# Attention and state space heads issued in pairs: scores of different rows in turn, transposes evicted by kind, products with v together

## The chip, the cores and the metric

One core of one Trainium2 chip runs the whole program in one launch. The metric is the device time of an execution in microseconds; the time of a kernel is the median of its runs.

## The reference

256 tokens of width 1024, batch 1, float32. The first block has two layers; each is a modulated RMS norm, a hybrid mixer, a residual, another norm, a squared-ReLU MLP, a residual. The mixer has three branches side by side, and the change touches all three:

```python
# differential attention: 4 heads, two maps of 32 columns each, v of 64
s1 = einsum('bqhd,bkhd->bhqk', q1b, k1) * scale; s2 = einsum(..., q2b, k2) * scale
p = _masked_softmax(s1, mask) - lam * _masked_softmax(s2, mask)
o = einsum('bhqk,bkhe->bqhe', p, v)
# MLA: 4 heads, scores from a 64-column and a 32-column (rotary) part, v of 64
sc = (einsum('bqhd,bkhd->bhqk', qnb, kn) + einsum('bqhr,bkr->bhqk', qrb, kr)) * scale
o = einsum('bhqk,bkhe->bqhe', _masked_softmax(sc, _chunk_mask(start, s)), v)
# state space (Mamba2): 8 heads of 64, state 64, two groups
scores = einsum('bclhn,bcshn->bhcls', cc, bc) * exp(where(causal, seg, -inf))
y_diag = einsum('bhcls,bcshp->bclhp', scores, xd)
```

The chunk mask lets a query see its own chunk of 64 keys and all earlier ones. The second block has one layer: a mixer of RWKV, moba attention (8 heads of 64 with ALiBi slopes, causal; with 256 tokens there is one block of keys) and an S5 state space branch, then a mixture of 32 experts.

## The kernel before

A class `Prog` emits the program; the Tile framework's scheduler orders each engine's instructions ahead of time by priorities and dependencies, which program order sets. Where `self.ordered` is on (`inorder`, `pin`), an instruction keeps its place in program order. So the code's order moves instructions, but the order on each engine is fixed before the run.

The large projections are "strips": a weight unit of 128 x 1024 comes by DMA (`raw`), ACT rounds it (`whi`), DVE takes the rest (`wlo`), and PE makes three products for each of eight blocks of 128 x 128 into a PSUM tile of tag `d` (`ps_d<-u,whi`, `ps_d<-xh,whi`, `ps_d<-u,wlo`). They stand between the attention steps. In the output projection they read `yh`/`xl` and accumulate into tiles of the tags `s` and `t`. The adaptive modulation's products (`ps_d<-raw,cnd_s`) are 32 columns wide, four column tiles beside each other.

PSUM in a mixer has eight banks: tags `d`, `s`, `t`, `o` with two each. One attention head or map goes like this:
- `scores` (L925): q against k into a tile of 128 x 384 of tag `s`, 128 columns for the first half of the queries and 256 for the second; head h reads rows 64a (MLA, moba) or 64a + 32m (diff) of the array. MLA adds a rotary product of 32 rows. `chunkmask` (L919) adds the mask with two bf16 products of one row.
- `soft` (L910): two reduces (L913, L914) and a scaling on DVE, two exps with sums on ACT (L378). A reciprocal and two multiplies on DVE follow; in diff attention two maps are combined with lambda (L1188 ff.).
- `pv` (L930): three transposes of 128 x 128 on PE (`tr`, L401) into a tile of tag `t`, one copy of 384 columns on ACT (`at_pT`), and two products with v into one half of the columns of `ps_o`.

`mla_head` (L1130) runs this four times one after the other; the diff loop (L1175) eight times, two maps to a `pv`; `moba` (L1641) eight times, with two slope products `mb_ak` of two rows and two masks of 128 rows in place of the chunk mask. The state space loop (L1225) goes head by head: an exponent product of 40 rows (`ps_s<-cs,i`), two masks, three exps (`ssE`), a multiply by `G` on DVE, two products with `xd` into one half of `ps_o`.

Every matmul goes through `mm` (L393), every ACT operation through `act` (L378, L379), DVE operations through `tt`, `ts`, `stt` (L382, L386, L390). So groups have these lines, and are told apart by their tiles.

Of the kernel before, what the change touches and what calls it, by code (L numbers as in the profile page):

```python
# [26 lines left out]
BF = mybir.dt.bfloat16  # L27
I32 = mybir.dt.int32
AF = mybir.ActivationFunctionType
OP = mybir.AluOpType  # L30
# [4 lines left out]
P = 128  # L35
T = 256
# [275 lines left out]
class Prog:  # L312
# [33 lines left out]
    def sb(self, pool, shape, tag, dt=F32, bufs=None):  # L346
        return pool.tile(shape, dt, name=tag, tag=tag, bufs=bufs)
# [568 lines left out]
        self.act(e[:, 0:P], sc[:, 0:P], AF.Exp, bias=mx[:, 0:1], scale=scale, accum=sm[:, j:j + 1])  # L916
        self.act(e[:, P:384], sc[:, P:384], AF.Exp, bias=mx[:, 1:2], scale=scale, accum=sm[:, j + 1:j + 2])

    def chunkmask(self, sc, r):  # L919

        for o in (0, 256):
            self.mm(sc[:, o:o + P], self.B("cm_q")[r:r + 1], self.B("cm_k")[r:r + 1], start=False, stop=True,
                    skip_group_check=True)

    def scores(self, sc, q, k, first, last=False):  # L925

        self.mm(sc[:, 0:P], q[:, 0:P], k[:, 0:P], start=first, stop=last, skip_group_check=True)
        self.mm(sc[:, P:384], q[:, P:T], k[:, 0:T], start=False, stop=last, skip_group_check=True)

    def pv(self, pool, p, v, vcol, o, half):  # L930

        tp = self.pt([P, 384], "t")
        for b in range(3):
            self.tr(tp[:, b * P:(b + 1) * P], p[:, b * P:(b + 1) * P])
        pT = self.sb(pool, [P, 384], "at_pT", bufs=2)

        self.act(pT, tp)
        oo = o[64 * half:64 * half + 64]
        self.mm(oo[:, 0:T], v[:, 0, vcol:vcol + 64], pT[:, 0:T], start=True, stop=False)
        self.mm(oo[:, P:T], v[:, 1, vcol:vcol + 64], pT[:, T:384], start=False, stop=True)  # L940


    def mixconst(self, l):
# [28 lines left out]
    def _mixer(self, pool, l, xT, pre, fill, n):  # L972
        nc = self.nc
        sb = lambda *a, **k: self.sb(pool, *a, **k)
# [4 lines left out]
        first = [("in", l) + k for k in names]  # L979
        sq = sb([P, 8, T], "yh")  # L980
        up, rs, _ = self.begin(xT, pre, l, 0, U, sq, first, "sstddt")
# [13 lines left out]
        for s in range(3):  # L995
            sq = sb([P, T], "pn_t", bufs=4)
            self.act(sq, cq[:, s], AF.Square)
            o = 0 if s < 2 else 2
            for i in range(2):
                self.mm(psn[:, o + i:o + i + 1], sq[:, i * P:(i + 1) * P], self.C("ones")[:, 0:1],  # L1000
                        start=(s == 0 and i == 0), stop=(s >= 1), skip_group_check=True)
# [13 lines left out]
        for s in range(3):  # L1015
            t = sb([P, T], "pn_t", bufs=4)
            g = self.col(f"qg{l}", s) if s < 2 else self.col(f"kvg{l}", 0)
# [24 lines left out]
        qn = sb([P, 2, T], "qn")  # L1042
        kn = sb([P, 2, T], "kn")
# [83 lines left out]
        sc96 = 96.0 ** -0.5  # L1127
        o = None

        def mla_head(h, o):  # L1130
            s, a = divmod(h, 2)
            sc = self.pt([P, 384], "s")
            r0 = slice(64 * a, 64 * a + 64)
            r1 = slice(32 * h, 32 * h + 32)
            self.scores(sc, qn[r0, s], kn[r0, s], True)
            self.scores(sc, qr[r1], krr[r1], False)
            self.chunkmask(sc, 32 * h)
            e = sb([P, 384], "at_e", bufs=3)
            sm = sb([P, 4], "at_s", bufs=3)
            self.soft(pool, sc, sc96, e, sm, 0)  # L1140
            nc.vector.reciprocal(sm[:, 0:2], sm[:, 0:2])
            self.ts(e[:, 0:P], e[:, 0:P], sm[:, 0:1], None, OP.mult)
            self.ts(e[:, P:384], e[:, P:384], sm[:, 1:2], None, OP.mult)
            self.pv(pool, e, vb, 64 * h, o, a)

        for s in range(2):
            o = self.pt([P, T], "o")
            for a in range(2):
                mla_head(2 * s + a, o)
            self.hl(yh[:, 2 + s], yl[:, 2 + s], o)  # L1150
            strip(("q", s), qa[:, s])
            strip(("k", s), ka[:, s])
# [21 lines left out]
        nsq = sb([P, 4, T], "nsq")  # L1174
        for s in range(2):  # L1175
            o = self.pt([P, T], "o")
            for a in range(2):
                sm = sb([P, 4], "at_s", bufs=3)
                es = []
                for m in range(2):  # L1180
                    sc = self.pt([P, 384], "s")
                    r = slice(64 * a + 32 * m, 64 * a + 32 * m + 32)
                    self.scores(sc, qa[r, s], ka[r, s], True)
                    self.chunkmask(sc, 64 * a + 32 * m)
                    e = sb([P, 384], "at_e", bufs=3)
                    self.soft(pool, sc, sc32, e, sm, 2 * m)
                    es.append(e)
                nc.vector.reciprocal(sm, sm)  # L1188
                self.ts(sm[:, 2:4], sm[:, 2:4], lam[:, 0:1], None, OP.mult)
                for i, c in ((0, slice(0, P)), (1, slice(P, 384))):  # L1190
                    self.ts(es[1][:, c], es[1][:, c], sm[:, 2 + i:3 + i], None, OP.mult)
                    self.stt(es[0][:, c], es[0][:, c], sm[:, i:i + 1], es[1][:, c], OP.mult, OP.add)
                self.pv(pool, es[0], va, 64 * (2 * s + a), o, a)
            nc.vector.tensor_copy(oa[:, s], o)
            self.act(nsq[:, s], o, AF.Square)
        pns = self.pt([P, 8], "t")
# [27 lines left out]
        nsq = sb([P, 4, T], "nsq")  # L1224
        for s in range(4):  # L1225
            po = self.pt([P, T], "o")
            for a in range(2):
                h = 2 * s + a
                pe = self.pt([P, 384], "s")
                neg, idb = self.B("causnegT"), self.B("ident")  # L1230
                self.mm(pe, self.i8[0:40, h:h + 1].to_broadcast([40, P]), cs, start=True, stop=False,
                        skip_group_check=True)
                self.mm(pe[:, 0:P], idb, neg, start=False, stop=True, skip_group_check=True)
                self.mm(pe[:, T:384], idb, neg, start=False, stop=True, skip_group_check=True)
                E = sb([P, 384], "ssE", bufs=2)
                self.act(E[:, 0:P], pe[:, 0:P], AF.Exp, bias=nA[:, h:h + 1])
                self.act(E[:, P:T], pe[:, P:T], AF.Exp, bias=nA[:, 16 + h:17 + h])
                self.act(E[:, T:384], pe[:, T:384], AF.Exp, bias=nA[:, 8 + h:9 + h])
                self.tt(E, E, G[:, h // 4], OP.mult)
                oo = po[64 * a:64 * a + 64]  # L1240
                self.mm(oo, xd[:, 0, h], E[:, 0:T], start=True, stop=False, skip_group_check=True)
                self.mm(oo[:, P:T], xd[:, 1, h], E[:, T:384], start=False, stop=True,
                        skip_group_check=True)
            self.stt(yc[:, s], xbc[:, 2 + s], self.col(f"dskip{l}", s), po, OP.mult, OP.add)
            self.stt(yc[:, s], yc[:, s], 0.5, zs[:, s], OP.mult, OP.mult)
            self.act(nsq[:, s], yc[:, s], AF.Square)
# [394 lines left out]
    def moba(self, pool, X, y):  # L1641
        nc = self.nc
        sb = lambda *a, **k: self.sb(pool, *a, **k)
        v = sb([P, 2, 512], "mb_v")
        ps = self.tokmajor(("tm2", 2816), X, 8, 512, 2)
        for i in range(2):
            self.act(v[:, i], ps[i])
        for s in range(4):
            q = sb([P, T], "mb_q", bufs=2)
            ps = self.strip(("in2", 1792 + P * s), X)  # L1650
            self.act(q, ps)
            k = sb([P, T], "mb_k", bufs=2)
            ps = self.strip(("in2", 2304 + P * s), X)
            nc.vector.tensor_copy(k, ps)
            o = self.pt([P, T], "o")
            for a in range(2):
                h = 2 * s + a
                r = slice(64 * a, 64 * a + 64)
                sc = self.pt([P, 384], "s")
                self.scores(sc, q[r], k[r], True)  # L1660
                aq, ak = self.B("al_q"), sb([2, T], "mb_ak", BF, 2)
                self.ts(ak, self.B("al_k")[0:2], 2.0 ** -(h + 1), None, OP.mult)
                self.mm(sc[:, 0:P], aq[0:2, 0:P], ak[0:2, 0:P], start=False, stop=False, skip_group_check=True)
                self.mm(sc[:, P:384], aq[0:2, P:T], ak[0:2, 0:T], start=False, stop=False,
                        skip_group_check=True)
                for c in (0, 256):
                    self.mm(sc[:, c:c + P], self.B("ident"), self.B("causneg"), start=False, stop=True,
                            skip_group_check=True)
                e = sb([P, 384], "at_e", bufs=3)
                sm = sb([P, 4], "at_s", bufs=3)  # L1670
                self.soft(pool, sc, 0.125, e, sm, 0)
                nc.vector.reciprocal(sm[:, 0:2], sm[:, 0:2])
                self.ts(e[:, 0:P], e[:, 0:P], sm[:, 0:1], None, OP.mult)
                self.ts(e[:, P:384], e[:, P:384], sm[:, 1:2], None, OP.mult)
                self.pv(pool, e, v, 64 * h, o, a)
            self.hl(y[0][:, s], y[1][:, s], o)

    def rwkv_start(self, pool, tmp, X):
# [981 lines left out]
```

## Time and profile before

| | before |
|---|---|
| runs, us | 1461.76, 1461.97, 1469.58 |
| median, us | 1461.97 |
| profiled execution: its own time / span, us | 1464.17 / 1462.4 |
| mean granted TensorE clock | 0.979 |
| busy, us: PE / PEld / DVE / ACT / POOL | 1369.8 / 1124.7 / 868.5 / 649.4 / 81.4 |
| instructions | 26516 |
| read from HBM, MB / mean GB/s | 306.46 / 212 |

The profiled execution's own time is 1.8 us more than its span, since some work lies around what the profiler records. Busy times of matmuls overlap, since they are pipelined: what a group costs is read from the start of one group to the start of the next. In layer 0 the edited stretch (from the first MLA scores to the output projection's start) lies at 85.9 to 172 us, in layer 1 at 460 to 546.5; moba at 885 to 935.

### The profile page before, as it was taken

The numbers are of one execution on the slowest core, as the hardware profiler recorded it, in microseconds if no ns is written. First come the engines' busy times: TensorE is split into PE (matmuls) and PEld (weight loads), VectorE is DVE, ScalarE is ACT, GpSimd is POOL, SyncE is SP. The second block draws the span as 40 slices with busy tenths as digits, with TensorE's granted clock in tenths as the row PEclk, the third lists the DMA queues.
The fourth block names the chain that finished last, engine by engine and source line by source line (L and its number), as shares of the span: only waits on it lengthen the run. The fifth ranks groups of instructions, "written<-read, shape, count | busy, mean of one in ns | idle before, by whom it ended". The sixth has DMA issues, their size and how long they took to land. (4 is left out here: it accounts for less than half of the span.)

```text
span 1462.4 us, 26516 instructions
## 1 busy us (share of the span) xinstructions
PE 1369.8 (94%) x10795; PEld 1124.7 (77%) x10795; DVE 868.5 (59%) x1983; ACT 649.4 (44%) x1295; POOL 81.4 (6%) x128
## 2 busy tenths in 40 slices
PE   4999999999999999899998989999998999999996
PEld 1787788999988878898997978888987864445442
DVE  2776677555588667998565465567746663222224
ACT  2655555444556545564555444355242432121121
POOL 0000000000000010023220010000000013000001
PEclk9999999999999999999999999999999999999998
DMA  9735467665565247444783333232124969999980
GB/s 371 295 140 202 186 247 278 224 252 198 178 259 197 89 176 268 156 159 171 186 233 115 116 104 143 89 145 87 59 92 159 405 218 366 420 410 375 399 327 30
DMA packets 45999, 311.71 MB, mean 213 GB/s; under 512 B 5296, under 2 KB 5744, under 8 KB 9648
## 3 DMA queue, kind: packets, MB, share of 16 engines
q1 hardware_dynamic: 41264, 293.10, 52.9%
q0 software_dynamic: 3312, 13.50, 3.5%
q10 hardware_dynamic: 1296, 3.36, 0.6%
q8 instruction: 87, 1.43, 0.4%
q14 instruction: 40, 0.33, 0.1%
HBM read 306.46 MB, written 3.47 MB: 212 GB/s over the span
## 5 line engine op out<-in xcount | busy, mean ns | idle before, releaser
L382 DVE TENSOR_TENSOR wlo<-raw,whi 128x1024 fp32r<-128x1024 f32 (+3 forms) x292 | 332.2, 1141 | 196.2 <-ACT whi L379 190.7
L379 ACT ACTIVATE whi<-raw 128x1024 fp32r<-128x1024 f32 (+3 forms) x292 | 284.5, 978 | 282.4 <-PE ps_d L393 202.4
L393 PE MATMUL ps_d<-xh,whi 128*128 128x256 f32 (+1 forms) x1072 | 310.8, 291 | 1.6 <-ACT whi L379 0.9
L393 PE MATMUL ps_d<-xh,wlo 128*128 128x256 f32 x816 | 234.3, 287 | 3.7 <-DVE wlo L382 3.6
L393 PE MATMUL ps_d<-xl,whi 128*128 128x256 f32 x816 | 232.9, 285 | 0.0
L393 PEld LDWEIGHTS ps_d<-xh,whi 128*128 128x128 f32 x1072 | 207.3, 193 | 7.6 <-issue 2.7
L393 PEld LDWEIGHTS ps_d<-xh,wlo 128*128 128x128 f32 x816 | 155.9, 191 | 6.9 <-DVE wlo L382 5.1
L393 PEld LDWEIGHTS ps_d<-xl,whi 128*128 128x128 f32 x816 | 155.9, 191 | 1.5 <-issue 1.2
L393 PE MATMUL ps_q<-ml_l,whi 128*128 128x256 f32 x512 | 145.6, 285 | 5.3 <-DVE ml_l L382 5.2
L393 PE MATMUL ps_q<-ml_h,whi 128*128 128x256 f32 x512 | 144.5, 285 | 6.3 <-DVE s5thr L390 4.8
L393 PE MATMUL ps_q<-ml_h,wlo 128*128 128x256 f32 x512 | 144.9, 284 | 0.0
L393 PE MATMUL ps_d<-raw,xg 128*64 128x512 f32 x488 | 110.0, 595 | 1.3 <-DVE xg L387 1.3
L393 PEld LDWEIGHTS ps_q<-ml_h,whi 128*128 128x128 f32 x512 | 97.3, 191 | 7.6 <-issue 7.0
L393 PEld LDWEIGHTS ps_q<-ml_l,whi 128*128 128x128 f32 x512 | 97.8, 191 | 6.6 <-DVE ml_l L382 6.6
L393 PEld LDWEIGHTS ps_q<-ml_h,wlo 128*128 128x128 f32 x512 | 97.7, 191 | 0.0
L393 PEld LDWEIGHTS ps_d<-raw,xg 128*64 128x64 f32 x488 | 34.1, 137 | 68.9 <-issue 65.8
L390 DVE SCALAR_TENSOR_TENSOR ex_t<-ex_t,ps_d 128x256 f32<-128x256 f32 x16 | 6.7, 421 | 135.0 <-ACT ex_t L379 135.0
L393 PE MATMUL ps_d<-u,whi 128*128 128x258 f32 x256 | 75.8, 301 | 0.0
L393 PE MATMUL ps_d<-u,wlo 128*128 128x258 f32 x256 | 70.7, 295 | 0.3 <-DVE wlo L382 0.3
L393 PE MATMUL ps_d<-raw,cnd_s 128*32 128x256 f32 x768 | 53.9, 415 | 12.4 <-DVE cnd_s L386 10.5
L379 ACT ACTIVATE ex_t<-ps_d 128x256 f32<-128x256 f32 x16 | 6.1, 383 | 128.7 <-PE ps_d L393 128.7
L393 PE MATMUL ps_y<-raw,ex_hT 128*64 128x512 f32 x256 | 57.7, 592 | 0.0
(777 smaller groups left out, 2632.7 us busy)
## 6 DMA issues: line engine op xcount, KB each, us to landing
raw<-W SPq DMA_DIRECT2D x277, 1024.0 KB, 7.3
s5TP<-s5kd POOLq DMA_DIRECT2D x8, 256.0 KB, 10.6
th<-rows POOLq DMA_DIRECT2D x2, 1024.0 KB, 8.6
raw<-W SPq DMA_DIRECT2D x4, 512.0 KB, 10.2
xT<-xT ACTq DMA_DIRECT2D x1, 1024.0 KB, 20.2
xd<-xT POOLq DMA_DIRECT2D x1, 1024.0 KB, 4.8
th<-W POOLq DMA_DIRECT2D x1, 1024.0 KB, 5.0
xg<-W POOLq DMA_DIRECT2D x1, 1024.0 KB, 6.5
```

What stands on the lines that cost most here:

```text
L379: return self.pin(self.nc.scalar.activation(out, in_, f, bias=bias, scale=scale))
L382: return self.pin(self.nc.vector.tensor_tensor(out, a, b, op=op))
L390: return self.pin(self.nc.vector.scalar_tensor_tensor(out, a, s, b, op0=op0, op1=op1))
L393: i = self.nc.tensor.matmul(out, l, r, start=start, stop=stop, **k)
```

## The change

`scores` and `chunkmask` take two heads and issue their products in turn, the second head first, pinned in this order on PE. `pv` becomes a generator for a pair: it takes the two heads' maps as they are ready, transposes them into two tiles by kind (`pa`: the first two blocks of both heads, `pb`: the third), copies each once (`at_pT` of 512 columns, `at_pU` of 256), and issues the two heads' products with v in turn, into both halves of `ps_o`. MLA: the second pair's scores, on tag `t`, are issued ahead of the first pair's transposes. Diff: the scores of two heads, four maps, are issued first, on tags `s` and `t`. State space: two heads' exponent products, exps, one multiply by G over 768 columns, then the products with xd in turn. Moba: q times k in turn, then slopes and masks head after head. The number of matmuls is the same.

On PE, in layer 0, at the first MLA scores (`kn,qn` are the 64-row parts, `krr,qr` the rotary ones, `c0b` holds the mask), the order before:

```order
L393 MATMUL ps_s<-kn,qn 128x128
L393 MATMUL ps_s<-kn,qn 128x256
L393 MATMUL ps_s<-krr,qr 128x128
L393 MATMUL ps_s<-krr,qr 128x256
L393 LDWEIGHTS c0b
L393 MATMUL ps_s<-c0b 128x128
L393 LDWEIGHTS c0b
L393 MATMUL ps_s<-c0b 128x128
L393 MATMUL ps_s<-kn,qn 128x128
L393 MATMUL ps_s<-kn,qn 128x256
```

and now:

```order
L393 MATMUL ps_s<-kn,qn 128x128 x2
L393 MATMUL ps_s<-kn,qn 128x256 x2
L393 MATMUL ps_s<-krr,qr 128x128 x2
L393 MATMUL ps_s<-krr,qr 128x256 x2
L393 LDWEIGHTS c0b
L393 MATMUL ps_s<-c0b 128x128
L393 LDWEIGHTS c0b
L393 MATMUL ps_s<-c0b 128x128
L393 LDWEIGHTS c0b
L393 MATMUL ps_s<-c0b 128x128
L393 LDWEIGHTS c0b
L393 MATMUL ps_s<-c0b 128x128
```

Two heads that stood one after the other now alternate; the same twelve rows follow on `ps_t` for the second pair, and only then the first pair's transposes.

On PE, in the state space heads of layer 0 (`cs,i` is the exponent product, `c0b` the mask, `yh` and `xl` are strips of the output projection), the order before:

```order
L393 MATMUL ps_o<-ssE,xd 64x256
L393 MATMUL ps_o<-ssE,xd 64x128
L393 MATMUL ps_s<-cs,i_122 128x384
L393 LDWEIGHTS c0b
L393 MATMUL ps_s<-c0b 128x128
L393 LDWEIGHTS c0b
L393 MATMUL ps_s<-c0b 128x128
L393 MATMUL ps_t<-yh,whi 128x256
L393 MATMUL ps_t<-xl,whi 128x256
L393 MATMUL ps_t<-yh,wlo 128x256
L393 MATMUL ps_o<-ssE,xd 64x256
L393 MATMUL ps_o<-ssE,xd 64x128
```

and now:

```order
L393 MATMUL ps_o<-ssE,xd 64x256 x2
L393 MATMUL ps_o<-ssE,xd 64x128 x2
L393 MATMUL ps_s<-cs,i_122 128x384
L393 LDWEIGHTS c0b
L393 MATMUL ps_s<-c0b 128x128
L393 LDWEIGHTS c0b
L393 MATMUL ps_s<-c0b 128x128
L393 LDWEIGHTS c0b
L393 MATMUL ps_s<-c0b 128x128
L393 MATMUL ps_o<-ssE,xd 64x256 x2
L393 MATMUL ps_o<-ssE,xd 64x128 x2
L393 MATMUL ps_s<-cs,i_122 128x384
```

The strips that stood between heads are gone from here, and the products of two heads follow each other.

The diff, cut:

```diff
+    def scores(self, sc, q, k, first):
+        two = list(zip(sc, q, k))[::-1]
+        with self.inorder(1):
+            for s, a, b in two:
+                self.mm(s[:, 0:P], a[:, 0:P], b[:, 0:P], start=first, stop=False, skip_group_check=True)
+            for s, a, b in two:
+                self.mm(s[:, P:384], a[:, P:T], b[:, 0:T], start=False, stop=False, skip_group_check=True)
...
+    def pv(self, pool, v, vcol, o, tag="t"):
+        pa, pb = self.pt([P, 2, T], tag), self.pt([P, 2, P], tag)
+        for a in range(2):
+            p = yield
+            for b in range(2):
+                self.tr(pa[:, a, b * P:(b + 1) * P], p[:, b * P:(b + 1) * P])
+            self.tr(pb[:, a], p[:, T:384])
+        ta, tb = self.sb(pool, [P, 2, T], "at_pT"), self.sb(pool, [P, 2, P], "at_pU")
+        self.act(ta, pa)
+        self.act(tb, pb)
...
+        for a in range(2):
+            self.mm(oo[a][:, 0:T], v[:, 0, c[a]], ta[:, a], start=True, stop=False, skip_group_check=True)
+        for a in range(2):
+            self.mm(oo[a][:, P:T], v[:, 1, c[a]], tb[:, a], start=False, stop=True, skip_group_check=True)
...
-        def mla_head(h, o):
...
+        def mla_scores(s):
+            sc = [self.pt([P, 384], "st"[s]) for _ in range(2)]
...
+        sc = mla_scores(0)
         for s in range(2):
+            e = [mla_soft(sc.pop(0)) for _ in range(2)]
+            if s == 0:
+                sc = mla_scores(1)
             o = self.pt([P, T], "o")
...
+            f = self.pv(pool, vb, 128 * s, o, "st"[s])
...
         for s in range(2):
             o = self.pt([P, T], "o")
+            g = "st"[s], "ts"[s]
+            sc = []
+            for a in range(2):
+                r = [64 * a, 64 * a + 32]
+                sc.append([self.pt([P, 384], g[a]) for _ in range(2)])
+                self.scores(sc[a], [qa[i:i + 32, s] for i in r], [ka[i:i + 32, s] for i in r], True)
+                self.chunkmask(sc[a], r)
...
             po = self.pt([P, T], "o")
+            E = sb([P, 2, 384], "ssE", bufs=2)
+            pe = [self.pt([P, 384], "s") for _ in range(2)]
...
+            self.tt(E, E, G[:, s // 2:s // 2 + 1].to_broadcast([P, 2, 384]), OP.mult)
+            for a in range(2):
+                self.mm(po[64 * a:64 * a + 64], xd[:, 0, 2 * s + a], E[:, a, 0:T], start=True, stop=False,
                         skip_group_check=True)
...
+            sc = [self.pt([P, 384], "s") for _ in range(2)]
+            r = [slice(64 * a, 64 * a + 64) for a in range(2)]
+            self.scores(sc, [q[i] for i in r], [k[i] for i in r], True)
```

## Rows read from the trace of the kernel before

**Rows 1.** The page, part 1: busy time, share of the span, instructions of each engine.
```profile
PE 1369.8 (94%) x10795; PEld 1124.7 (77%) x10795; DVE 868.5 (59%) x1983; ACT 649.4 (44%) x1295; POOL 81.4 (6%) x128
```

**Rows 2.** Table by window: length, busy us (x instructions) of PE, PEld, DVE, ACT, POOL; PEclk; DMA share; GB/s.
```profile
85.90:172.00 86.10, 85.83 (x638) 66.48 (x638) 53.14 (x151) 44.97 (x131) 0.29 (x3) 0.96 0.45 172
460.00:546.50 86.50, 85.72 (x625) 69.26 (x624) 56.29 (x151) 46.17 (x132) 4.38 (x3) 0.98 0.35 133
885.00:935.00 50.00, 49.43 (x361) 40.73 (x359) 26.03 (x72) 23.65 (x60) 0.00 (x0) 1.00 0.29 105
```

**Rows 3.** PE timeline, MLA scores, layer 0: start, busy us, engine, line, operation, out<-in, tile, shape, passes.
```profile
85.90 0.92 PE L393 MATMUL ps_s<-kn,qn 64*128 64x128 f32 x4
86.75 0.92 PE L393 MATMUL ps_s<-krr,qr 32*128 32x128 f32 x4
...
87.71 0.92 PE L393 MATMUL ps_s<-kn,qn 64*128 64x128 f32 x4
```

**Rows 4.** PE timeline, one diff map, strips after it, one head's product with v.
```profile
129.13 0.92 PE L393 MATMUL ps_s<-ka,qa 32*128 32x128 f32 x4
...
130.09 0.39 PE L393 MATMUL ps_d<-u,wlo 128*128 128x258 f32 x1
130.31 0.28 PE L393 MATMUL ps_d<-u,whi 128*128 128x258 f32 x1
130.43 0.28 PE L393 MATMUL ps_d<-xh,whi 128*128 128x258 f32 x1
...
132.98 0.86 PE L393 MATMUL ps_o<-at_pT,va 128*64 128x256 f32 x4
133.78 0.39 PE L393 MATMUL ps_d<-xh,whi 128*128 128x258 f32 x1
```

**Rows 5.** PE timeline, two diff maps that stood close together.
```profile
134.09 1.03 PE L393 MATMUL ps_s<-ka,qa 32*128 32x128 f32 x7
134.85 0.27 PE L393 MATMUL ps_s<-c0b 1*128 1x128 bf16 x2
...
135.27 0.55 PE L401 MATMUL ps_t<-c,at_e 128*128 128x128 f32 x3
135.75 0.28 PE L393 MATMUL ps_s<-c0b 1*128 1x128 bf16 x2
135.96 0.39 PE L393 MATMUL ps_d<-u,wlo 128*128 128x258 f32 x1
```

**Rows 6.** PE timeline, products with v of two moba heads that met.
```profile
901.56 0.93 PE L393 MATMUL ps_o<-at_pT,mb_v 128*64 128x256 f32 x8
```

**Rows 7.** ACT groups, layer 0 mixer: count, busy us, mean ns, idle before and its releaser.
```profile
L379 ACT ACTIVATE whi<-raw 128x1024 fp32r<-128x1024 f32 x11 | 11.6, 1058 | 7.6 <-PE ps_d L393 7.5
...
L379 ACT ACTIVATE at_pT<-ps_t 128x384 f32<-128x384 f32 x8 | 3.8, 488 | 6.8 <-PE ps_t L401 6.8
```

**Rows 8.** DVE groups, layer 0 mixer.
```profile
L382 DVE TENSOR_TENSOR wlo<-raw,whi 128x1024 fp32r<-128x1024 f32 x12 | 14.6, 1219 | 6.3 <-ACT whi L379 6.3
...
L382 DVE TENSOR_TENSOR ssE<-ssE,G 128x384 f32<-128x384 f32 x8 | 4.4, 553 | 1.0 <-ACT ssE L379 1.0
```

**Rows 9.** DVE timeline, the combining of a diff head, then the reduces of the next.
```profile
128.86 0.17 DVE L1188 RECIPROCAL at_s<-at_s 128x4 f32<-128x4 f32 x1
...
129.33 0.55 DVE L386 TENSOR_SCALAR at_e<-at_e,at_s 128x128 f32<-128x128 f32 x2
...
130.45 0.28 DVE L913 TENSOR_REDUCE at_mx<-ps_s 128x1 f32<-128x128 f32 x1
...
131.10 0.17 DVE L386 TENSOR_SCALAR at_mx<-at_mx 128x2 f32<-128x2 f32 x1
```

**Rows 10.** ACT timeline, exps of one diff map; then of two state space heads.
```profile
126.08 0.36 ACT L378 ACTIVATE at_e<-ps_s,at_mx 128x128 f32<-128x128 f32 x1
...
126.78 0.20 ACT L378 ACTIVATION_READ_ACCUMULATOR at_e<-ps_s,at_mx 128x1 f32 x1
...
155.25 1.66 ACT L379 ACTIVATE ssE<-ps_s,nA 128x128 f32<-128x128 f32 x6 [2.68 <-PE ps_s L393]
```

More of the change, by code (lines that the diff above doesn't have):

```diff
@@ L917, in soft @@
         self.act(e[:, P:384], sc[:, P:384], AF.Exp, bias=mx[:, 1:2], scale=scale, accum=sm[:, j + 1:j + 2])
[L919 to L940, printed above, removed]
+    def chunkmask(self, sc, rows):
+        with self.inorder(1):
+            for o in (0, 256):
+                for s, r in list(zip(sc, rows))[::-1]:
+                    self.mm(s[:, o:o + P], self.B("cm_q")[r:r + 1], self.B("cm_k")[r:r + 1], start=False, stop=True,
+                            skip_group_check=True)
@@ new lines, in scores @@
+    def scores(self, sc, q, k, first):
+        two = list(zip(sc, q, k))[::-1]
+        with self.inorder(1):
+            for s, a, b in two:
[12 more added lines that the diff above has]
+        self.act(tb, pb)
+        oo = [o[64 * a:64 * a + 64] for a in range(2)]
+        c = [slice(vcol + 64 * a, vcol + 64 * a + 64) for a in range(2)]
+        for a in range(2):
+            self.mm(oo[a][:, 0:T], v[:, 0, c[a]], ta[:, a], start=True, stop=False, skip_group_check=True)
+        for a in range(2):
+            self.mm(oo[a][:, P:T], v[:, 1, c[a]], tb[:, a], start=False, stop=True, skip_group_check=True)
+        yield
@@ L1128, in _mixer, with mla_soft @@
         o = None
-        def mla_head(h, o):
[L1131 to L1137, printed above, removed]
+        def mla_scores(s):
+            sc = [self.pt([P, 384], "st"[s]) for _ in range(2)]
+            r0 = [slice(64 * a, 64 * a + 64) for a in range(2)]
+            r1 = [slice(64 * s + 32 * a, 64 * s + 32 * a + 32) for a in range(2)]
+            self.scores(sc, [qn[r, s] for r in r0], [kn[r, s] for r in r0], True)
+            self.scores(sc, [qr[r] for r in r1], [krr[r] for r in r1], False)
+            self.chunkmask(sc, [64 * s, 64 * s + 32])
+            return sc
+        def mla_soft(sc):
             e = sb([P, 384], "at_e", bufs=3)
@@ L1143, in mla_head @@
             self.ts(e[:, P:384], e[:, P:384], sm[:, 1:2], None, OP.mult)
-            self.pv(pool, e, vb, 64 * h, o, a)
+            return e
+        sc = mla_scores(0)
         for s in range(2):
+            e = [mla_soft(sc.pop(0)) for _ in range(2)]
+            if s == 0:
+                sc = mla_scores(1)
             o = self.pt([P, T], "o")
-            for a in range(2):
-                mla_head(2 * s + a, o)
+            f = self.pv(pool, vb, 128 * s, o, "st"[s])
+            next(f)
+            while e:
+                f.send(e.pop(0))
+            f = None
             self.hl(yh[:, 2 + s], yl[:, 2 + s], o)
@@ L1180, in _mixer @@
                 for m in range(2):
[L1181 to L1184, printed above, removed]
                     e = sb([P, 384], "at_e", bufs=3)
-                    self.soft(pool, sc, sc32, e, sm, 2 * m)
+                    self.soft(pool, sc[a].pop(0), sc32, e, sm, 2 * m)
                     es.append(e)
@@ L1192, in _mixer @@
                     self.stt(es[0][:, c], es[0][:, c], sm[:, i:i + 1], es[1][:, c], OP.mult, OP.add)
-                self.pv(pool, es[0], va, 64 * (2 * s + a), o, a)
+                if a == 0:
+                    f = self.pv(pool, va, 128 * s, o, g[0])
+                    next(f)
+                f.send(es[0])
+            f = e = es = sc = None
             nc.vector.tensor_copy(oa[:, s], o)
@@ L1226, in _mixer @@
             po = self.pt([P, T], "o")
+            E = sb([P, 2, 384], "ssE", bufs=2)
+            pe = [self.pt([P, 384], "s") for _ in range(2)]
+            neg, idb = self.B("causnegT"), self.B("ident")
+            for a in (1, 0):
+                h = 2 * s + a
+                self.mm(pe[a], self.i8[0:40, h:h + 1].to_broadcast([40, P]), cs, start=True, stop=False,
+                        skip_group_check=True)
             for a in range(2):
                 h = 2 * s + a
-                pe = self.pt([P, 384], "s")
@@ L1230, in _mixer @@
-                neg, idb = self.B("causnegT"), self.B("ident")
-                self.mm(pe, self.i8[0:40, h:h + 1].to_broadcast([40, P]), cs, start=True, stop=False,
-                        skip_group_check=True)
[L1233 to L1242, printed above, removed]
+                self.mm(pe[a][:, 0:P], idb, neg, start=False, stop=True, skip_group_check=True)
@@ new lines, in _mixer @@
+                self.mm(pe[a][:, T:384], idb, neg, start=False, stop=True, skip_group_check=True)
+            for a in range(2):
+                h = 2 * s + a
+                for c, b in ((slice(0, P), 0), (slice(P, T), 16), (slice(T, 384), 8)):
+                    self.act(E[:, a, c], pe[a][:, c], AF.Exp, bias=nA[:, b + h:b + h + 1])
+            self.tt(E, E, G[:, s // 2:s // 2 + 1].to_broadcast([P, 2, 384]), OP.mult)
+            for a in range(2):
+                self.mm(po[64 * a:64 * a + 64], xd[:, 0, 2 * s + a], E[:, a, 0:T], start=True, stop=False,
+                        skip_group_check=True)
@@ L1243, in _mixer @@
+            for a in range(2):
+                self.mm(po[64 * a:64 * a + 64, P:T], xd[:, 1, 2 * s + a], E[:, a, T:384], start=False, stop=True,
                         skip_group_check=True)
+            pe = None
             self.stt(yc[:, s], xbc[:, 2 + s], self.col(f"dskip{l}", s), po, OP.mult, OP.add)
@@ L1655, in moba @@
             o = self.pt([P, T], "o")
-            for a in range(2):
[L1657 to L1664, printed above, removed]
+            sc = [self.pt([P, 384], "s") for _ in range(2)]
+            r = [slice(64 * a, 64 * a + 64) for a in range(2)]
+            self.scores(sc, [q[i] for i in r], [k[i] for i in r], True)
+            aq = self.B("al_q")
+            self.ordered = 1
+            for a in range(2):
+                ak = sb([2, T], "mb_ak", BF, 2)
+                self.ts(ak, self.B("al_k")[0:2], 2.0 ** -(2 * s + a + 1), None, OP.mult)
+                self.mm(sc[a][:, 0:P], aq[0:2, 0:P], ak[0:2, 0:P], start=False, stop=False, skip_group_check=True)
+                self.mm(sc[a][:, P:384], aq[0:2, P:T], ak[0:2, 0:T], start=False, stop=False,
                         skip_group_check=True)
+            for a in range(2):
                 for c in (0, 256):
-                    self.mm(sc[:, c:c + P], self.B("ident"), self.B("causneg"), start=False, stop=True,
+                    self.mm(sc[a][:, c:c + P], self.B("ident"), self.B("causneg"), start=False, stop=True,
                             skip_group_check=True)
+            self.ordered = 0
+            f = self.pv(pool, v, 128 * s, o)
+            next(f)
+            for a in range(2):
                 e = sb([P, 384], "at_e", bufs=3)
                 sm = sb([P, 4], "at_s", bufs=3)
-                self.soft(pool, sc, 0.125, e, sm, 0)
+                self.soft(pool, sc[a], 0.125, e, sm, 0)
                 nc.vector.reciprocal(sm[:, 0:2], sm[:, 0:2])
@@ L1674, in moba @@
                 self.ts(e[:, P:384], e[:, P:384], sm[:, 1:2], None, OP.mult)
-                self.pv(pool, e, v, 64 * h, o, a)
+                f.send(e)
+            f = e = sc = None
             self.hl(y[0][:, s], y[1][:, s], o)
```

## The prediction

> **What bounds the kernel now.** I read the first part of the page, then tables by window, then the PE timeline. The page gives PE 94% of the span, DVE 59%, ACT 44% [rows 1]. That is a mean over stages, so the three stages that the change edits come next: the mixers of layers 0 and 1 (86.1 and 86.5 us) and the moba stage (50.0 us) [rows 2]. In each PE is busy for some 99%, DVE for 52 to 65%, ACT for 47 to 53%, and the DMA share is 0.29 to 0.45. So PE's own work is the bound there, the chains of attention and state space lie beneath other matmuls, and a microsecond less on PE is a microsecond less of span as long as PE stays fed. The reader is to look at two things: what the small matmuls cost PE, from the start of one group to the start of the next (busy times overlap), and how long the chains on ACT and DVE are that PE must cover meanwhile.
>
> The granted clock is 0.96 and 0.98 in the mixers [rows 2]: full speed but for stretches at half, which cost 0.04 × 86.1 = 3.4 and 0.02 × 86.5 = 1.7 us. I take them as unchanged; a stretch more or less lies in the range.
>
> **What it removes: matmul time.** The number of matmuls stays. An fp32 matmul is two passes in the timeline, so four passes are one head's two score products.
>
> *Scores of MLA.* One head, from its first pass to the next head's, takes 87.71 − 85.90 = 1.81 us [rows 3]; eight heads in two layers, 14.5. What two heads cost together the trace shows at the diff scores, where two of them met by chance [rows 5]: 135.27 − 134.09 = 1.18 plus 135.96 − 135.75 = 0.21 for the second head's masks, 1.39 us, against 130.09 − 129.13 = 0.96 for one [rows 4]. There the last pass of the second head stood behind the first one's masks. For passes strictly in turn I take the price of one head plus a little for the masks: 1.9 us for an MLA pair, 1.0 for a diff pair. The bounds are 1.39/0.96 of one head (2.6 us for an MLA pair, 2.9 us less gain over four pairs) and exactly one head (0.4 us more). 14.5 − 4 × 1.9 = **6.9 us**.
>
> *Scores of diff.* Sixteen maps, of which three pairs already ran as in [rows 5]: 10 × 0.96 + 3 × 1.39 = 13.8, afterwards 8 × 1.0: **5.8 us**. The pairs of two heads now stand next to each other, on four different groups of rows; if those overlapped too, it would be up to 3 us more.
>
> That passes overlap across a mask which stands between them in program order is what [rows 5] shows: seven score passes start from 134.09 on, the first head's masks only at 134.85. The Trainium skill (TensorE: Matmul & The Clock Gate, Part 3) says that matmuls keep program order in start and end; by that rule no two heads overlap in the kernel before, and the diff scores would win 16 × 0.96 − 8.0 = 7.4 us instead of 5.8. The trace decides against it here.
>
> *Products with v.* A single head takes 133.78 − 132.98 = 0.80 us [rows 4], busy for 0.86; two heads that met are busy for 0.93 [rows 6], so I take 0.87 for a pair. Of 24 heads (MLA, diff and moba, 8 each) sixteen ran single and eight in four pairs: 16 × 0.80 + 4 × 0.87 = 16.3, afterwards 12 × 0.87 = 10.4: **5.9 us**.
>
> *State space products xd.* They have the shapes of the products with v, 0.80 us a head. 16 × 0.80 = 12.8, afterwards 8 × 0.87 = 7.0: **5.8 us**. The exponent products (40 rows each) share their rows and stay.
>
> *Moba scores.* The q·k part has the shape of MLA's first part, 86.75 − 85.90 = 0.85 us a head [rows 3]; slope products and masks stay on the same rows. 8 × 0.85 − 4 × 0.85 = **3.4 us**.
>
> *Returns from a small tile to the full array.* The first full matmul after one takes 130.31 − 130.09 = 0.22 us to its successor, the next 130.43 − 130.31 = 0.12 [rows 4]: 0.10 a return. The order on PE has 73 of them in the three stages before and 52 after: 21 × 0.10 = **2.1 us**.
>
> Sum on PE: 6.9 + 5.8 + 5.9 + 5.8 + 3.4 + 2.1 = **29.9 us**.
>
> **What it adds on ACT and DVE: nearly nothing.** A pair's transposes leave by copies of 512 and 256 columns instead of twice 384. One of 384 takes 488 ns, one of 1024 (another line, from SBUF) 1058 [rows 7]; by that slope they take 0.60 and 0.38, 0.98 us, which is 2 × 0.49. The multiply by G of 768 columns should be about 0.95, by the same kind of slope between 553 ns for 384 and 1219 for 1024 columns [rows 8], against 2 × 0.55. Neither is on the path while PE has strips (the 128-row products of the projections) beside them.
>
> **What it moves: the waits.** Until now a head's chain lay beneath the next head's scores. Now PE issues a pair at once, and the chains of two heads come due together. One softmax map, from its scores to its transposes: reduces and scaling 130.45 to 131.27, 0.82; exps with their accumulator reads 126.08 to 126.98, 0.90; reciprocal 0.17; multiplies 0.55; together 2.4 us [rows 9, 10]. The second head comes 0.9 later (ACT), the copies out of PSUM take 0.98: 4.3 us for a pair of MLA or moba. Diff: 0.82 + two maps of 0.90 + combining 130.45 − 128.86 = 1.59, 4.2 us a head [rows 9, 10], with 0.98 of copies a pair. State space: six exps 1.66 [rows 10] and the multiply 0.95, 2.6 a pair. With nothing to cover them: 8 × 4.3 + 8 × 4.2 + 4 × 0.98 + 8 × 2.6 = 93 us, the far bound; the near one is 0.
>
> The order on PE tells the cover, at 0.12 us a strip matmul [rows 4]. *MLA*, first pair: the second pair's scores (with masks about 2.2 us) stand ahead of the transposes and leave 2.4 − 2.2 = 0.2; 3 strips against 0.9 leave 0.5, and 5 against 0.98 leave 0.4. The second pair has more strips, I allow 0.3: 1.4 a layer. *Diff*, first pair of heads: the second score pair (1.0) and 25 strips (3.0) cover the 4.2 but for 0.2, the copies have 0.6 of 0.98: 0.6 in all. Second pair: the other scores and 22 strips cover 1.0 + 2.6 of 4.2, and a weight split of 1.22 [rows 8] stands ahead of these reduces on DVE: 1.8; then twenty 32-row products, put at half a strip each (1.2), against 1.8 of the other head's exps, 0.6, and 0.4 at the copies: 2.8. Together 3.4 a layer. *State space*: in layer 0 no strip is left between the four pairs. A pair's own work on PE is 0.87 for xd and what I put at 1.2 for two exponent products with their masks, its chain 2.6: 4 × 0.5 and a first wait of 0.5 are 2.5; in layer 1 26 strips remain, I take 1.5. *Moba*: 32 strips (3.8) cover 2.4; the last pair's six transposes stand together at the end: 0.8. Sum: 2 × 1.4 + 2 × 3.4 + 2.5 + 1.5 + 0.8 = **14.4 us**, 15% of 93.
>
> **The sum.** The durations come from the profiled execution, which took 1464.17 us: 1464.2 − 29.9 + 14.4 = 1448.7. The median of the runs, 1461.97, lies 2.2 below it, so I predict **1446.5 us**. A measurement of this kernel can tell some 0.5% from no change, 7.3 us: faster means below 1454.7, slower above 1469.3. What follows these stages is not edited, and I take the saved time to reach the end.
>
> **Rivals.**
> - *The gain is whole.* PE stays fed, since there are strips for each wait. For it: PE idles for about 1% now, with chains as long [rows 2]. Against: the state space pairs of layer 0 with no strip between. Stalls of 2 us: 1464.2 − 29.9 + 2 − 2.2 = 1434.
> - *The gain is eaten.* The slow passes that go were the cover. For it: ACT and DVE are each half busy in these stages [rows 2], with weight splits of 1.06 and 1.22 us [rows 7, 8] in order between the softmax steps, and a step that meets one waits that long. At 30% uncovered: 1464.2 − 29.9 + 28 − 2.2 = 1460. The Trainium skill (TensorEngine Tiling (Array Packing), Performance Considerations) speaks for this one: packing speeds up TensorE but not the evacuation of PSUM, which may then be the bottleneck. No run here shows it.
> - *Slower: bare chains.* At the diff and state space pairs both `s` tiles of PSUM are taken at once, so the next pair's first matmul waits until this pair's exps have left them on ACT. It decides from 30/93, a third of the chains uncovered; at half it is 1464.2 − 29.9 + 46.5 − 2.2 = 1479. Against it: layer 0 alone has pairs without strips.
> - *It doesn't do what it says.* If passes of two heads didn't overlap in fixed order, only the 2.1 us of returns would be won and the waits paid: 1464.2 − 2.1 + 14.4 − 2.2 = 1474. [Rows 5] and [rows 6] speak against it.
>
> **How the numbers follow.** Forecast (1440 to 1453) 0.55; whole gain (1430 to 1440) 0.18; eaten (1454 to 1469) 0.20; bare chains 0.05; no overlap 0.02. Faster is the first two, 0.73; same 0.20; slower 0.07. The range, 1433 to 1458, leaves out the best of the whole gain, the eaten case above 1458 and the two slow ones, about 0.2.
>
> **What would show it.** Right: eight passes of a pair in about 0.85 us from start to start; the three stages shorter by about 5, 6 and 5 us; PE idle ahead of at_e transposes in the diff heads and of xd products in layer 0. Wrong: pairs at 1.4 us or more (no overlap); PE below 95% in the mixers with reduces or exps as releasers (eaten, or bare chains); more stretches at half clock, for which no term here stands; or a difference in later stages, which the change doesn't edit.

## The result

The changed kernel takes 1444.49 us (median of four runs, 1442.13 to 1449.72); the kernel before, run beside it, 1463.82. The ratio is 0.9869, interval 0.9847 to 0.9891: 16 to 22 us faster. The forecast was 1446.5, in a range of 1433 to 1458, with 0.73 on faster. The profiled execution took 1442.13 us, 22.0 less than the one of before.

The page of the changed kernel, part 1 (for [rows 1]):

```profile
span 1440.3 us, 26471 instructions
...
PE 1338.6 (93%) x10795; PEld 1106.4 (77%) x10795; DVE 868.6 (60%) x1975; ACT 645.6 (45%) x1295; POOL 81.1 (6%) x128
```

PE has the same 10795 matmuls and is busy for 31 us less. To see where, both kernels are cut at the same instructions: the mixers from the `ps_t<-c,dtA` products ahead of MLA to the last `pn_t` of the state space output, moba from the last strip ahead of it to rwkv's first product, and the S5 stage ahead of moba. The table by window, columns as in [rows 2]; the kernel before (layer 0, layer 1, moba, S5):

```profile
85.13:184.52 99.39, 99.11 (x748) 78.00 (x748) 63.28 (x175) 51.48 (x141) 0.29 (x3) 0.97 0.45 171
457.30:552.82 95.52, 93.22 (x685) 74.26 (x685) 64.27 (x172) 51.08 (x141) 4.71 (x3) 0.98 0.38 134
885.36:958.67 73.31, 71.68 (x540) 62.23 (x539) 41.05 (x96) 33.96 (x76) 0.00 (x0) 1.00 0.33 118
775.12:885.36 110.24, 97.66 (x722) 86.95 (x720) 62.50 (x114) 50.47 (x95) 8.70 (x17) 0.94 0.32 112
```

and the changed one:

```profile
84.17:172.18 88.01, 84.42 (x748) 68.43 (x748) 61.83 (x170) 49.88 (x141) 0.30 (x3) 0.96 0.52 193
444.49:532.54 88.05, 83.40 (x685) 68.40 (x685) 64.78 (x169) 49.96 (x141) 4.72 (x3) 0.94 0.41 144
867.99:936.10 68.11, 65.50 (x540) 58.90 (x539) 41.10 (x96) 32.98 (x76) 0.00 (x0) 1.00 0.36 127
755.34:867.99 112.65, 99.42 (x722) 88.00 (x721) 62.45 (x114) 50.50 (x95) 8.36 (x17) 0.91 0.31 110
```

The edited stages are shorter by 11.4, 7.5 and 5.2 us, 24.1 together; the S5 stage, not edited, is 2.4 longer, at a granted clock of 0.91 instead of 0.94. In the edited stages PE idles (length less busy time) for 0.3 + 2.3 + 1.6 = 4.2 us before and 3.6 + 4.6 + 2.6 = 10.8 now: waits have come in, less than the work that went.

How a pair runs now, PE timeline (columns as in [rows 3]), of layer 0 first: MLA pairs on `ps_s` and `ps_t`, the first transposes, four diff maps, a pair of products with v, one of xd; then a moba pair:

```profile
92.72 0.93 PE L393 MATMUL ps_s<-kn,qn 64*128 64x128 f32 x8
93.57 0.92 PE L393 MATMUL ps_s<-krr,qr 32*128 32x128 f32 x8
94.33 0.28 PE L393 MATMUL ps_s<-c0b 1*128 1x128 bf16 x4
94.54 1.48 PE L393 MATMUL ps_t<-kn,qn 64*128 64x128 f32 x8
95.95 0.92 PE L393 MATMUL ps_t<-krr,qr 32*128 32x128 f32 x8
96.70 0.28 PE L393 MATMUL ps_t<-c0b 1*128 1x128 bf16 x4
97.85 0.61 PE L401 MATMUL ps_s<-c,at_e 128*128 128x128 f32 x3 [0.86 <-DVE at_e L386]
...
119.54 0.71 PE L393 MATMUL ps_s<-ka,qa 32*128 32x128 f32 x6
119.88 0.37 PE L393 MATMUL ps_t<-ka,qa 32*128 32x128 f32 x1
...
120.30 0.28 PE L393 MATMUL ps_s<-c0b 1*128 1x128 bf16 x4
...
121.04 0.39 PE L393 MATMUL ps_d<-xh,whi 128*128 128x258 f32 x1
...
124.97 0.30 PE L401 MATMUL ps_s<-c,at_e 128*128 128x128 f32 x1 [0.68 <-DVE at_e L390]
...
129.33 0.65 PE L393 MATMUL ps_o<-at_pT,va 128*64 128x256 f32 x4
129.81 0.39 PE L393 MATMUL ps_o<-at_pU,va 128*64 128x128 f32 x4
130.13 0.71 PE L393 MATMUL ps_t<-ka,qa 32*128 32x128 f32 x6
...
136.75 0.30 PE L401 MATMUL ps_t<-c,at_e 128*128 128x128 f32 x1 [1.56 <-ACT un_c L379]
...
146.01 0.87 PE L393 MATMUL ps_o<-ssE,xd 128*64 128x256 f32 x8
146.81 0.43 PE L393 MATMUL ps_s<-cs,i 40*128 40x384 f32 x1
...
876.20 0.93 PE L393 MATMUL ps_s<-mb_k,mb_q 64*128 64x128 f32 x8
...
877.70 0.36 PE L393 MATMUL ps_d<-xh,wlo 128*128 128x256 f32 x1
```

Eight passes take what four took in [rows 3]: 93.57 − 92.72 = 0.85 us. Four diff maps with their masks take 121.04 − 119.54 = 1.50, since passes on `ps_t` (119.88) begin before those on `ps_s` and their masks (120.30) are done: four maps deep. A pair of products with v takes 0.80, one of xd 0.80, a moba pair with slopes and masks 1.50. The second MLA pair takes 2.4 instead of 1.8. The bracketed numbers are PE's idle time ahead of transposes: 0.86, 0.68 and 1.56.

### The profile page after: what moved, and what is told of

The parts are those of the page before. It is cut to its first block, busy times and chain, and to the rows that moved or that the text cites. A ratio compares the mean times of both kernels' runs of the same rounds, so it can differ in the third digit from the quotient of the medians.

```text
span 1440.3 us, 26471 instructions
## 1 busy us (share of the span) xinstructions
PE 1338.6 (93%) x10795; PEld 1106.4 (77%) x10795; DVE 868.6 (60%) x1975; ACT 645.6 (45%) x1295; POOL 81.1 (6%) x128
```

## The experiments

Single executions scatter: ten of the changed kernel lie between 1440.5 and 1449.7 us, with mean clocks of 0.978 down to 0.964. So parts are judged by the lengths of the stages, with the time at half clock (1.2 GHz) beside them; half of that time is the most that it can have cost. Medians decide only differences of 6 us or more. The stages are those above; the two kernels of "Strips between" and "Dummy products" below stand in the text, since some 20 of their passes fall behind the cut that ends layer 1's mixer.

| kernel | median, us | layer 0 / layer 1 / moba, us | of it at half clock, us |
|---|---|---|---|
| before | 1463.8 | 99.4 / 95.5 / 73.3 | 6.8 / 3.4 / 0 |
| changed | 1444.5 | 88.0 / 88.1 / 68.1 | 6.8 / 10.2 / 0 |
| e1_ssm_single | 1442.6 | 89.1 / 87.4 / 68.2 | 0 / 3.4 / 0 |
| e2_heads_whole | 1455.8 | 92.9 / 94.1 / 75.7 | 10.2 / 17.1 / 10.2 |
| e3_pv_by_head | 1450.4 | 94.3 / 86.8 / 70.2 | 10.2 / 0 / 0 |
| e4_moba_before | 1442.4 | 91.1 / 89.2 / 73.3 | 13.7 / 13.7 / 0 |
| f3_adjacent | 1439.9 | 88.8 / 87.6 / 69.0 | 6.8 / 6.8 / 0 |
| f4_no_norm | 1433.9 | 84.9 / 83.6 / 67.1 | 0 / 3.4 / 0 |
| i1_changed_again | 1448.5 | 88.1 / 88.1 / 68.2 | 6.8 / 10.2 / 0 |
| i2_ssm_single_again | 1451.1 | 95.4 / 91.0 / 74.2 | 17.1 / 13.7 / 13.7 |
| i3_mla_strips_ssm_single | 1467.9 | 100.5 / 95.7 / 74.3 | 20.5 / 13.7 / 13.7 |
| i4_mla_strips | 1464.5 | 99.2 / 95.5 / 74.3 | 27.3 / 20.5 / 13.7 |

**Whole heads one after the other.**

```diff
-            for s, a, b in two:  # first products of both, second of both
+            for n in (1, 0):     # products and masks of one head, then of the other
```

> The changed kernel with each head's scores issued whole (its products, then its masks) before the next head's; all else as changed. Theory A (it is the alternation that lets two heads' passes run together): an MLA pair 2.6 instead of 1.82 us, four diff maps 2.8 instead of 1.3, moba pairs 1.3 instead of 0.85 for q times k: 4 x 0.8 + 4 x 1.5 + 4 x 0.4 = 11 us more, 1453 to 1457. Rival B (adjacency alone does it, passes overlap across masks): at most 4 us more, below 1449. Rival C (no overlap at all without alternation): 21 us more, about 1465.

11.3 us slower in the median, as A said, but not by A's sum. Part of it is the clock: the stages are 18.4 us longer together, with 20.5 us more at half clock, up to 10.2 of the 18.4. The PE timeline of this kernel, both MLA pairs, then diff, then a moba pair:

```profile
94.62 0.92 PE L393 MATMUL ps_s<-kn,qn 64*128 64x128 f32 x4
95.47 0.92 PE L393 MATMUL ps_s<-krr,qr 32*128 32x128 f32 x4
96.23 0.27 PE L393 MATMUL ps_s<-c0b 1*128 1x128 bf16 x2
96.43 0.92 PE L393 MATMUL ps_s<-kn,qn 64*128 64x128 f32 x4
...
100.70 0.42 PE L393 MATMUL ps_t<-c0b 1*128 1x128 bf16 x2
101.05 1.65 PE L393 MATMUL ps_t<-kn,qn 64*128 64x128 f32 x4
...
128.10 1.03 PE L393 MATMUL ps_s<-ka,qa 32*128 32x128 f32 x7
...
130.05 0.39 PE L393 MATMUL ps_d<-xh,whi 128*128 128x258 f32 x1
...
889.09 0.92 PE L393 MATMUL ps_s<-mb_k,mb_q 64*128 64x128 f32 x4
...
890.43 0.92 PE L393 MATMUL ps_s<-mb_k,mb_q 64*128 64x128 f32 x4
...
891.64 0.36 PE L393 MATMUL ps_d<-xh,wlo 128*128 128x256 f32 x1
```

MLA heads don't overlap at all (96.43 − 94.62 = 1.81, C's case), nor do moba's (890.43 − 889.09 = 1.34, the pair 2.55); diff maps partly, 1.95 us for four instead of 1.50, as in [rows 5]. So what stands between two 64-row heads keeps them apart: rotary products and masks in MLA, slopes and masks in moba. Shared rows are not the whole reason. In the second MLA pair the first head's rotary products and masks lie on rows 96 to 127 and the next head's first part on rows 0 to 63, and it still begins only behind the masks (101.05 after 100.70, here at half clock). Which property of the products between decides, no run separates. The clock fell to half for 10.2 us after 4.2 us of these MLA scores.

**Adjacent, but not in turn.**

```diff
             for s, a, b in two:
                 self.mm(s[:, 0:P], ...)
-            for s, a, b in two:
                 self.mm(s[:, P:384], ...)
```

> The changed kernel with the same order on PE except inside the pairs: both products of one head, then both of the other (scores, products with v, xd), masks of both after them. Theory A (adjacency is enough, PE starts passes of other rows early): score pairs from start to start within 0.2 us of 0.85, the whole within 2 us of the changed kernel. Theory C (the product in turn is what matters): a score pair at 1.2 us or more and a pair of products with v at 1.2 or more, 0.4 us x (12 score pairs + 4 rotary pairs + 12 + 8 pairs of products) = 14 us slower, about 1458.

Theory A. This kernel's first MLA pair:

```profile
94.56 0.93 PE L393 MATMUL ps_s<-kn,qn 64*128 64x128 f32 x8
95.42 0.93 PE L393 MATMUL ps_s<-krr,qr 32*128 32x128 f32 x8
```

95.42 − 94.56 = 0.86, as in turn. The stages are within 1 us each, the time is no longer (1439.9). It is the nearness of the two heads, with nothing else between, that counts.

**Products with v head by head.** `pv` with its three transposes, one copy of 384 columns and two products for each head, as in the kernel before.

> The changed kernel with transposes, one copy of 384 columns and products with v head by head as before; scores and state space as changed. Theory A: twelve pairs at 0.80 become twenty-four heads at 0.80, plus 9.6, and twelve more returns to the full array, plus 1.2; shorter waits for the copies give back 2: 7 to 11 us slower, 1451.5 to 1455.5. Rival B (the copies of a pair are what PE waits for, so the gain of the products is spent there): less than 3 us slower.

5.9 us slower in the median, 2.1 in moba at full clock in both, and in the mixers 6.3 with 3.4 us more at half clock and −1.2 with 10.2 less; with half of that time taken off, 4.6 and 3.9. Together the stages give 7.2 as they stand and 10.6 with the clock taken off, within A's 7 to 11; the median is below it.

**Moba as before.**

> The changed kernel with the moba stage as before. Theory A (each stage's gain stands by itself): the 5.2 us by which the moba stage is shorter in the profile come back, 1448.5 to 1451. Rival B (the stage only inherits time from elsewhere, a clock stretch or a transfer): less than 2 us.

The stage is 73.29 us again, 5.2 longer, as A said. The median doesn't show it (1442.4): the scatter is as large as this part.

**State space heads one by one**, twice, the second time beside the unaltered changed kernel.

```diff
-            pe = [self.pt([P, 384], "s") for _ in range(2)]
+            for a in range(2):
+                pe = self.pt([P, 384], "s")
```

> The changed kernel (1444.5 us) with the state space heads one by one as before; everything else as changed. Theory A (passes of two heads run together, part of that is given back in waits): sixteen xd heads at 0.80 us in place of eight pairs at 0.80 to 0.87, plus 6; waits at the pairs go, minus 2: 3 to 5 us slower than the changed kernel, 1447.5 to 1449.5. Rival B (the stretches at half clock that lie in this section in both layers of the changed kernel, 6.8 us each, come from the pairing, and go with it, 3.4 us a layer): within 2 us of the changed kernel, and both mixers show full clock there.

> The changed kernel with the state space heads one by one, once more with more rounds. Theory A (the pairing of these heads is worth its 5.8 us of matmul time less waits): 3 to 6 us slower than the unaltered changed kernel of this call. Rival B (what the pairing saves on PE is spent in waits and in half-clock stretches that fall in its section): within 2 us, or faster.

> The changed kernel itself, unaltered, beside the next three on the same chip. Its time moves with the stretches at half clock: both theories expect 1442 to 1449.

The two together don't tell it apart: 1442.6 against 1444.5, then 1451.1 against 1448.5. B's claim on the clock falls: the second time this kernel has half-clock stretches in the state space heads too, and its layer 0 takes 95.4 us where the first took 89.1 at full clock, the same instructions. At full clock the pairing is worth at most 89.1 − (88.0 − 3.4) = 4.5 us in layer 0. Whether it pays in the end stays open.

**Strips between the state space pairs**: two of the four z strips moved into the loop's first two passes.

> The changed kernel with two of the four z strips moved in the code from ahead of the state space loop into its first two passes, so that strips stand between the pairs on PE; nothing is left out. Theory A (the pairs of the state space have too little beside them: PE waits for exps, and the stretches at half clock fall there): the 1.7 us wait ahead of the last diff head's transposes and 0.5 to 1 us of small waits go in each layer, and the stretch at half clock in this section goes (3.4 us a layer): 5 to 9 us faster than the changed kernel, 1435.5 to 1439.5. Rival B (the strips only change places and the diff chains, which they covered, come bare; the clock falls elsewhere): within 3 us of the changed kernel.

1446.05 us, ratio 0.9881 against 0.9869: B. The wait of 1.56 is gone, but PE now waits for exps (`ssE`) for 0.86 and 0.48 us, the wait at the diff transposes stays, and the clock still fell to half in this section for 6.8 us. Layer 0 takes 87.9 us with 6.8 us at half clock, as in the changed kernel. The time as a whole is a weaker witness, since a wait for a weight unit came up behind layer 1's mixer, where the changed kernel has none (PE timeline):

```profile
533.85 1.94 PE L393 MATMUL ps_d<-raw,cnd_s 128*32 128x256 f32 x16 [4.10 <-DMA raw<-W]
```

Why that transfer landed later was not tested.

**Dummy products beside the state space pairs.**

> The changed kernel with four full-array fp32 products (128 x 256, result unused) put in with each pair of state space heads, 16 a layer, 0.21 us each, 3.4 us a layer if nothing else changes. Theory A (the clock falls there because the array does too little): no half-clock stretch in the state space section of either layer (3.4 us a layer back) and waits of about 1 us covered: within 2 us of the changed kernel. Rival B (the stretches at half clock have nothing to do with what PE does there): stretches as before, and 5 to 7 us slower, about 1450.

1458.98 us, 14.5 slower, neither A's time nor B's. The expectation had the price of a product wrong. Its PE timeline, four products of layer 0 and what follows them, then the place behind layer 1's mixer:

```profile
151.87 1.95 PE L393 MATMUL ps_d<-oa,c 128*128 128x256 f32 x8
153.74 0.43 PE L393 MATMUL ps_s<-cs,i 40*128 40x384 f32 x1
...
546.26 0.62 PE L393 MATMUL ps_d<-raw,cnd_s 128*32 128x256 f32 x2 [4.30 <-DMA raw<-W]
```

Each product is two passes, and four take 153.74 − 151.87 = 1.87 us, 0.47 each instead of 0.21: some 15 us for all 32, an estimate from these four. The wait for a weight unit, 4.30 us, is here too. No half-clock stretch lies in the state space heads of either layer, as A said; one of 3.4 us lies just ahead of them in layer 0. That the dummies kept the clock up is not shown by it: the first kernel with state space heads one by one has no such stretch there either, without dummies.

**Without normalisation.** It leaves out the reciprocals, the multiplies by them and lambda's scaling.

> The changed kernel without the softmax normalisation: reciprocals, multiplies by them and lambda's scaling are left out in MLA, diff and moba, so each chain on DVE is shorter by about 0.7 us (MLA, moba) to 0.9 us (diff). Theory A (the idle PE ahead of the at_e transposes is these chains): PE idle ahead of at_e transposes, about 3.6 us in layer 0, falls by half or more; edited stages shorter by 1 to 2 us each. Rival B (the idle time there is ACT's: exps and weight splits in order): the idle time stays within 0.5 us.

10.6 us faster, by two executions. PE's idle time ahead of the at_e transposes, groups of PE by line in layer 0 (columns as in [rows 7]), first the changed kernel:

```profile
L401 PE MATMUL ps_t<-c,at_e 128*128 128x128 f32 x12 | 2.8, 288 | 1.6 <-ACT un_c L379 1.6
...
L401 PE MATMUL ps_s<-c,at_e 128*128 128x128 f32 x12 | 2.7, 295 | 1.5 <-DVE at_e L386 0.9 <-DVE at_e L390 0.7
```

then without normalisation:

```profile
L401 PE MATMUL ps_t<-c,at_e 128*128 128x128 f32 x12 | 2.6, 284 | 0.9 <-DVE at_mx L386 0.9
L401 PE MATMUL ps_s<-c,at_e 128*128 128x128 f32 x12 | 2.6, 295 | 1.3 <-DVE at_mx L386 0.7 <-ACT at_e L378 0.6
```

3.1 became 2.2, not half; in moba 1.3 became 0.4. With a shorter chain the planner also puts the transposes earlier, and PE then waits for what remains. The chains are the cause in part. Over the three stages PE's idle time fell only from 10.8 to 9.3 us, while 13.7 us less ran at half clock: of the 8.7 us by which the stages are shorter, up to 6.8 are clock.

**Strips pinned into MLA's wait**, with state space heads single (i3) and in pairs (i4).

```diff
-            strip(("q", s), qa[:, s])        # after pv
+            with self.inorder(1):            # ahead of pv's transposes
+                strip(("q", s), qa[:, s])
```

> State space heads one by one, and in MLA the next strip's 24 matmuls pinned ahead of the pair's transposes, so that PE has work while the softmax chain runs. Theory A (the 1.0 us of idle PE in each layer's MLA is an order that puts transposes too early, and strips cover it): 2 us less than the kernel with state space heads one by one alone, and no idle PE at MLA's transposes in the profile. Rival B (the wait only moves to the copies or the next pair): within 0.5 us by the stage's length.

> The changed kernel with the same pin in MLA, state space in pairs. Theory A: 2 us less than the unaltered changed kernel, by the lengths of the two mixers at equal clock. Rival B: no difference, the wait moves.

1467.94 and 1464.52 us: all of the gain lost. The wait ahead of MLA's transposes is gone, and this stands ahead of it (PE timeline of i4, then the table by window of the stretch at half clock):

```profile
85.32 0.84 PE L393 MATMUL ps_t<-c,dtA 128*40 128x128 f32 x4
88.01 1.64 PE L401 MATMUL ps_t<-c,xbc 128*128 128x128 f32 x6 [1.85 <-DVE nA L382]
92.31 0.69 PE L401 MATMUL ps_t<-c,xbc 128*128 128x128 f32 x2 [2.66 <-DVE xbc L390]
```

```profile
88.08:105.15 17.07, 14.41 (x73) 10.81 (x74) 9.75 (x30) 3.50 (x16) 0.19 (x2) 0.50 0.14 56
```

In the changed kernel 56 strip passes stand between the first and the last of these three groups and cover the convolution chain on DVE; with 24 of them pinned behind MLA's scores, none is left here. To save 0.9 us, 4.5 us of idle PE came in, and with it 17 us at half clock. Both theories missed this. Not all of the loss is shown to be the pin's: moba, which it doesn't touch, is 6.2 us longer too, with 13.7 us at half clock. No complete version here beats the changed kernel by more than the scatter.

## Why the prediction was right

The mechanism and the sign were right, and the time is 2.0 us off; by their own rows the terms were less exact, and the errors partly cancel. Part of the nearness is luck: the sum was set on a median of 1461.97 us for the kernel before, which with the later run is 1463.82, so that a net gain forecast as 15.5 and measured as 19.3 comes out only 2.0 off in the time.

- *MLA scores*, forecast 6.9: pairs of 1.8 and 2.4 (in the second a weight load waits 0.26 us for DVE's `xd`, which still reads from tiles of tag `t`): 14.5 − 2 × 4.2 = 6.1.
- *Diff scores*, 5.8: four maps in 1.50, 13.8 − 4 × 1.50 = 7.8. The bound "up to 3 us more" was nearer: neighbouring pairs do overlap.
- *Products with v*, 5.9, and *xd*, 5.8: 0.80 a pair instead of 0.87, 6.7 and 6.4.
- *Moba scores*, 3.4: with slopes and masks 4 × (2.55 − 1.50) = 4.2; 2.55 is a pair with whole heads in the first experiment. The forecast left slopes and masks as they were.
- *Returns*, 2.1: the order holds them; not measured apart.

On PE that is 33.3 instead of 29.9. *The waits*, forecast 14.4, were mis-sized most: PE idles 10.8 − 4.2 = 6.6 us more. Some places were right (MLA's first pair 0.9, diff 0.7 and 1.6 in layer 0), and strips covered more. One was not: of the 4.0 us forecast for the state space pairs none came in layer 0, where PE idles ahead of no xd product, a sign that the text had named; in layer 1 it is 0.7, two waits, of which the longer is

```profile
502.80 0.43 PE L393 MATMUL ps_s<-cs,i 40*128 40x384 f32 x1 [0.47 <-ACT ssE L379]
```

The heads of layer 0 ran at half clock for 6.8 us, and a slower PE leaves the exps more time; how much of that wait it covered is not shown. So the stages, forecast to be shorter by 5, 6 and 5 us, are shorter by 11.4, 7.5 and 5.2. A sign of being wrong came near as well: PE is busy for 94.7% of layer 1's mixer, below the 95% named, though mostly with multiplies as releasers and not reduces or exps. *The clock*, "taken as unchanged", was not: 17.1 us at half speed in the edited stages instead of 10.2, up to 3.4 us. 33.3 − 6.6 − 3.4 = 23.3, measured 24.1. The forecast net was 15.5 and the profiled pair shows 22; the medians 19.3. The S5 stage's 2.4 us is a half-clock difference in a part that wasn't edited, which the text had named as a sign against it; it goes with the clock in that stage.

Of the rivals, "whole gain" (1434) was nearer in its waits, 2 us against the 6.6 measured, than the forecast, but not in the time. "Eaten" and "bare chains" didn't come: 6.6 of 93 us lie bare. "No overlap" is refuted by the first rows. The Trainium skill (TensorE: Matmul & The Clock Gate, Part 3) says that matmuls keep program order in start and end; the trace doesn't agree, since passes on `ps_t` started at 119.88 us and the masks on `ps_s`, ahead of them in program order, at 120.30. Its picture of matmuls of other rows side by side is borne out, with 0.85 us for eight passes.

## What to carry to other kernels

Issue small matmuls of different row or column groups next to each other, with no other products between: order within the pair doesn't matter, masks and rotary or slope products between do. Before an order is tightened, look what else the displaced work was covering: i4 won 0.9 us and lost 4.5 in the chain ahead of it, and more by the clock. And judge parts of a few microseconds by stages and their clock, not by medians.

## What the runs showed of the hardware

Passes of four 32-row maps run side by side (1.50 us for four with masks, one alone 0.96 [rows 4]), also across one map's masks; 64-row heads with rotary products and masks between don't (1.81 each), even where these lie on other rows. The layer 0 of one kernel, state space heads one by one, took 89.1 and 95.4 us in two executions, with 0 and 17 us at 1.2 GHz. In i4 the fall came right after PE had idled 1.85 us and had begun on six transposes; in e2 after 4 us of MLA scores of single heads.
